# Where a two-layer trunk reduces its modulation weights, and when it draws its gate matmuls

## The chip, the cores and the metric

The program runs on one core of one Trainium2 chip. The metric is the device time of one execution in microseconds (us). The engines of the core are TensorE (PE in the rows), VectorE (DVE), ScalarE (ACT), GpSimd (POOL) and SyncE (SP), which issues the DMA transfers. Each engine runs its own instructions in a fixed order and waits at an instruction until what it needs is there.

## The reference

A trunk of two layers runs over 256 context tokens and 256 latent tokens of width 1024. In each layer the tokens are normalized and modulated, projected by `w_in`, and go through four mixers: grouped attention, a Hyena mixer (two gated long convolutions with filters from a small network), a pooling mixer and a gMLP mixer. Each mixer's result is projected back to the model's width, multiplied by a sigmoid gate that is itself a projection of the tokens, and added up; `w_out` and a SwiGLU feed-forward follow. Shifts, scales and gates of the modulation are a product of a vector with `w_mod`.

```python
mod = (act_lat @ w_mod[l] + b_mod[l])[:, None, :]
sh1, s1, g1, sh2, s2, g2 = jnp.split(mod, 6, axis=-1)
...
p = modulate(x, norm1_w[l], sh1, s1) @ w_in[l]
q = apply_rope(attn_q(p[..., Q_OFF:K_OFF], q_norm_w[l]), cos, sin)
...
# long_conv, twice in the Hyena mixer
uf = jnp.fft.rfft(u.astype(jnp.float32), n=2 * n, axis=1)
y = jnp.fft.irfft(uf * kf[None], n=2 * n, axis=1)[:, :n]
...
merged = (g[..., 0, :] * (attn_out @ lp['w_br_attn'])
          + g[..., 1, :] * (hy @ lp['w_br_hyena'])
          + g[..., 2, :] * (pl @ lp['w_br_pool'])
          + g[..., 3, :] * (gm @ lp['w_br_gmlp']))
x = x + g1 * (merged @ lp['w_out'])
x = x + g2 * swiglu(modulate(x, norm2_w[l], sh2, s2), ffn_w_gate[l], ffn_w_up[l], ffn_w_down[l])
```

The last layer uses its context tokens only for keys and values, so its other work runs over 256 tokens.

## The kernel before

All tokens stay on the chip, with the features on the partitions. The weights are streamed once, in units of 128 x 1024 numbers (512 KB). A product in fp32 is made of three matmuls: each operand is split into a high part and a low part, and `mm3` (L209 to L211) adds high x high, high x low and low x high in one accumulator, over 512 columns in layer 0 and mostly 256 in layer 1. For a weight unit, `load_next` issues a DMA of `raw` on SP's queue, ScalarE casts the high part `whi` (L171) and VectorE subtracts the low part `wlo` (L174). There are five raw buffers and four each of `whi` and `wlo`; a raw buffer is free for the next load when its unit has been split.

`unit_order` lists every unit in the order in which it is streamed, and with it the order of the work. In each layer come the wide units of keys, values and gMLP, ten narrow units (Hyena and pooling), then the gates. `gates(b, js)` gives for the mixer b and each of eight row blocks the gate unit `w_nar` and the projection `w_br`. The wide units of the queries stand between the gates of the gMLP mixer (3) and the others (2, 1, 0). Then come `w_out` (8 units) and the feed-forward in two halves: 22 units of `w_ff` (gate and up), 11 of `w_dn` (down).

The modulation is not computed on TensorE, but for a few chunks. Most of it is made of tiles `w_t`, units of 128 x 1024 too, which `mod_tile` multiplies with a broadcast vector and reduces on VectorE (L259), twice per tile, once for the context and once for the latent tokens. The function `mix(units, tiles)` spreads the tiles evenly between other units. `TILES0` (28 tiles of layer 0: the factor of the first residual, 16 to 23, and most of the feed-forward's modulation) lies in the gate stretch of layer 0, 68 units; `TILES1` (44 tiles of layer 1) lies in layer 0's feed-forward, between its sixth unit and the last four. A tile takes one of the five raw buffers until its reduces are done. The reduces keep the program's order among themselves.

Beside the main line of matmuls run generators. The gates are such a generator (`fill`), and `pump(n)` draws n halves of them (12 matmuls for a half of a gate unit in layer 0) at every `yield` of another generator, so that TensorE has work while the others wait for VectorE and ScalarE. `hyena_gen` draws `HRATE` at each `yield`: it makes the forward transforms (`psU`), the products with the filters' spectra (`ya`, `yb`, L1074 to L1076, split to `yh`, `yl` by L142 and L143), and the inverse transforms (`psiv`), for each of two orders. The query phase draws `QRATE[l]` in each of its steps: `q_gen` normalizes and turns the queries (`qr`, L782) and transposes them on TensorE (`psqT`, L827). `spectra_gen(1)` makes the spectra of layer 1's filters beside the last eight row blocks of layer 0's `w_dn`: exponentials, windows (`fo`, `fs`, `fd`, `fa`), their sum (`pstot`), a reciprocal (L508), products with it (L519), and transforms (`pssp`) of the split results (`fh`, `fl`).

`residual` (L1242) multiplies a finished row block (`pmk`, `pmd`) by its modulation and adds it to `x`, in two halves; `acc` (L322) gathers squares for the next norm.

Each engine's order is written by a scheduler that takes the program, the buffers and its own estimates of durations; the kernel itself fixes the order in which units are loaded and tiles are reduced.

Of the kernel before, what the change touches and what calls it, by code (L numbers as in the profile page):

```python
# [20 lines left out]
KT = D // P  # L21
# [21 lines left out]
BUB = (4, 1)  # L43
REST = 1

HRATE = (1.0, 1.0)
QRATE = (1.4, 1.3)
ARATE = (0.7, 1.4)
QN = (3, 4)
LAG = (1, 2)  # L50
# [2 lines left out]

TILES0 = [(0, i) for i in (*range(16, 24), *range(24, 40), *range(44, 48))]
TILES1 = [(1, i) for i in (*range(40), *range(44, 48))]
MODT = TILES0 + TILES1
CHUNKS = [(0, (8 + i, 9 + i, i, i + 1)) for i in range(0, 8, 2)]
CHUNKS += [(l, tuple(range(4 * c, 4 * c + 4))) for l, c in ((0, 10), (1, 10))]  # L60
# [6 lines left out]
def unit_order():  # L67


    def mix(units, tiles):  # L70
        r, n = [], 0
        for i, u in enumerate(units):
            r.append(u)
            while n * len(units) < (i + 1) * len(tiles):
                r.append(("w_t", MODT.index(tiles[n])))
                n += 1
        return r

    o = []
    for l in range(DEPTH):  # L80
        def gates(b, js):
            return [(n, l, j + (10 + b * KT if n == "w_nar" else 0)) for j in js for n in ("w_nar", f"w_br{b}")]

        o += [("w_wide", l, 0, u) for u in range(4)]
        o += [("w_nar", l, i) for i in range(10)]
        mid = gates(3, range(KT)) + [("w_wide", l, 1, u) for u in range(4)]
        mid += gates(2, range(KT)) + gates(1, range(KT)) + gates(0, range(KT))
        if l == 0:
            mid = mix(mid, TILES0)
        o += mid  # L90
        o += [("w_out", l, j) for j in range(KT)]
        ff = []
        for half in range(2):
            ff += [("w_ff", l, i, half * NFH + f) for f in range(NFH) for i in range(2)]
            ff += [("w_dn", l, half, u) for u in range(NFH)]
        if l == 0:
            ff = ff[:6] + mix(ff[6:-4], TILES1) + ff[-4:]
        o += ff
    return o
# [3 lines left out]
def trunk_kernel(ctx: ExitStack, tc: tile.TileContext, I, out: bass.AP):  # L103
# [543 lines left out]
    o = bank("ss")  # L647
# [7 lines left out]
    for l in range(DEPTH):  # L655
# [364 lines left out]
        def hyena_gen():  # L1020
# [32 lines left out]
            for od in range(2):  # L1053
# [5 lines left out]
                for f in range(2):  # L1059
                    us = []  # L1060
                    for im in range(2):
                        o = side("U")
                        col = im * 256 + f * P
                        for k in range(2):
                            h, lo = fwd[k]
                            mm3(
                                o[:, CS], h[:, col : col + P], lo[:, col : col + P],
                                ut[k][0][:, CS], ut[k][1][:, CS], k == 0, k == 1,
                            )
                        us.append(o)  # L1070
                    kc = "C0" if f == 0 else "A1"
                    for im, (ka, kb_, op) in enumerate(((f"A{f}", f"B{f}", ALU.subtract), (f"B{f}", kc, ALU.add))):
                        a, b = t2(s="ya"), t2(s="yb")
                        V.tensor_mul(seqs(a), seqs(us[0]), kb(ka))  # L1074
                        V.tensor_mul(seqs(b), seqs(us[1]), kb(kb_))
                        V.tensor_tensor(a[:, CS], a[:, CS], b[:, CS], op=op)  # L1076
                        hi, lo = t2(F32R, "yh"), t2(F32R, "yl")
                        split(hi[:, CS], lo[:, CS], a[:, CS])
                        ysp[2 * im + f] = (hi, lo)
                    yield  # L1080
                    yield
                order = (0, 2, 1, 3)
                if od == 0:
                    nut = []
# [46 lines left out]
            qs[t] = t2(s="qs")  # L1131
            S.copy(qs[t], os_[t])
        qg = q_gen()
        for _ in range(len(tts) + QN[l]):
            next(qg, None)
            pump(QRATE[l])

        att = {}

# [387 lines left out]
```

## Time and profile before

| | us |
|---|---|
| median of 3 runs | 1329.41 |
| lowest, highest | 1328.41, 1329.69 |
| profiled execution | 1328.54 |
| its span in the profile | 1326.0 |
| TensorE busy | 1292.9 |
| VectorE busy | 935.6 |
| ScalarE busy | 608.6 |

The rows further down are read so. A busy row gives for each engine the busy time, its share of the span and the number of instructions. A row of the waits names the engine and the operation that waited, the line, the engine and line that released it, the time in all, the times and the longest. A row of the windows gives a stretch, its length, then the busy time (and the count) of PE, PEld, DVE, ACT and POOL, the granted TensorE clock as a share of full speed, the busy share of the DMA engines, and GB/s. A row of a timeline gives start and duration, engine, line, operation, result and operands, shape and count, and in brackets the idle time before it and who ended it. Matmuls overlap: the time from one start to the next is what one costs.

### The profile page before, as it was taken

Reading aid. Unit: us, or ns where it says so; the run is one execution under the profiler, and the core shown is the slowest. Engines: PE = TensorE matmul, PEld = TensorE weight load, DVE = VectorE, ACT = ScalarE, POOL = GpSimd, SP = SyncE. Lnnn points to the kernel's source line nnn. Section 1 sums busy time; section 2 is a strip of 40 time slices with the busy share of each in tenths; the row PEclk is TensorE's granted clock in tenths of the full one; section 3 lists DMA queues with packets and bytes.
Section 4 is the critical chain, followed back from the end, with each engine's and each line's share of the span. In section 5 each row is a group of like instructions: output and inputs, shape, how many; then the busy total and the mean of one; then the engine's idle time right before and its main releaser. Section 6 shows DMA issues by size and latency. Waiting matters only on the chain.

```text
span 1326.0 us, 19996 instructions
## 1 busy us (share of the span) xinstructions
PE 1292.9 (98%) x7714; PEld 1128.2 (85%) x7714; DVE 935.6 (71%) x1599; ACT 608.6 (46%) x1060; POOL 61.9 (5%) x69
## 2 busy tenths in 40 slices
PE   4999999999999999999999999999999999999997
PEld 3778788888888887888888888889989999999997
DVE  3687788798987356666667767966889876655554
ACT  3564333367753246222222224365468854543443
POOL 0000500300000000000000000001210000000000
PEclk7999999999999999999999999999999999999999
DMA  9532334343245552554555554424434457455551
GB/s 343 210 127 77 104 104 143 126 143 112 93 157 160 174 209 73 173 164 159 174 174 175 182 168 143 159 80 128 134 110 139 151 192 247 159 179 188 179 187 49
DMA packets 68063, 203.85 MB, mean 154 GB/s; under 512 B 7552, under 2 KB 13824, under 8 KB 67968
## 3 DMA queue, kind: packets, MB, share of 16 engines
q1 hardware_dynamic: 67968, 202.58, 46.1%
q8 instruction: 60, 0.98, 0.3%
q14 instruction: 35, 0.29, 0.1%
HBM read 201.50 MB, written 1.05 MB: 153 GB/s over the span
## 4 chain that ended last, share of the span: by engine, by line
PE 75%; issue 16%; DVE 5%; ACT 2%; POOL 1%; DMA 0%; DVEq 0%; POOLq 0%; ACTq 0%
PE pmn L209 14%; PE pmn L211 14%; PE pmn L210 14%; PE pmd L209 3%; PE pmd L210 3%; PE pmd L211 3%; PE pmb L209 2%; PE pmb L210 2%; PE pmb L211 2%; PE pmw L676 2%; PE pmw L678 2%; PE pmw L677 2%; PE psav L1188 1%; PE pspt L1166 1%; DVE wlo L174 1%
## 5 line engine op out<-in xcount | busy, mean ns | idle before, releaser
L171 ACT CAST whi<-raw 128x1024 fp32r<-128x1024 f32 (+2 forms) x312 | 288.1, 929 | 470.8 <-PE pmn L210 214.4
L209 PE MATMUL pmn<-hh,whi 128*128 128x512 f32 (+1 forms) x1328 | 449.9, 339 | 0.3 <-DVE vst L721 0.3
L210 PE MATMUL pmn<-hl,whi 128*128 128x512 f32 (+1 forms) x1328 | 448.1, 337 | 0.0
L211 PE MATMUL pmn<-hh,wlo 128*128 128x512 f32 (+1 forms) x1328 | 447.7, 337 | 0.3 <-DVE wlo L174 0.3
L174 DVE TENSOR_TENSOR wlo<-raw,whi 128x1024 fp32r<-128x1024 f32 (+2 forms) x312 | 335.7, 1078 | 143.3 <-ACT whi L171 141.0
L211 PEld LDWEIGHTS pmn<-hh,wlo 128*128 128x128 f32 x1328 | 252.0, 190 | 27.7 <-issue 1.1
L209 PEld LDWEIGHTS pmn<-hh,whi 128*128 128x128 f32 x1328 | 252.1, 190 | 27.6 <-issue 0.9
L210 PEld LDWEIGHTS pmn<-hl,whi 128*128 128x128 f32 x1328 | 252.1, 190 | 26.0 <-issue 0.7
L259 DVE CUSTOM_DVE_ANT_0 junk<-raw,cb,pack_a 128x1024 bf16<-128x1024 f32 x144 | 187.0, 1299 | 1.4
L209 PE MATMUL pmd<-hh,whi 128*128 128x512 f32 (+1 forms) x352 | 119.2, 339 | 0.0
L210 PE MATMUL pmd<-hl,whi 128*128 128x512 f32 (+1 forms) x352 | 118.7, 337 | 0.0
L211 PE MATMUL pmd<-hh,wlo 128*128 128x512 f32 (+1 forms) x352 | 118.0, 336 | 0.0
L210 PEld LDWEIGHTS pmd<-hl,whi 128*128 128x128 f32 x352 | 66.8, 190 | 7.2 <-issue 0.5
L211 PEld LDWEIGHTS pmd<-hh,wlo 128*128 128x128 f32 x352 | 66.8, 190 | 7.1 <-issue 0.2
L209 PEld LDWEIGHTS pmd<-hh,whi 128*128 128x128 f32 x352 | 66.8, 190 | 7.1 <-issue 0.2
L1314 DVE TENSOR_TENSOR sg<-sg,pmn 128x512 f32<-128x512 f32 (+1 forms) x42 | 23.3, 554 | 65.0 <-PE pmn L211 65.0
L345 POOL TENSOR_TENSOR rs<-rs,halfexp 128x4 f32<-128x4 f32 (+1 forms) x5 | 4.4, 884 | 956.9 <-DVE rs L343 956.9
L676 PE MATMUL pmw<-whi,hh 128*128 128x512 f32 (+1 forms) x112 | 43.8, 392 | 3.8 <-ACT hh L389 3.8
L677 PE MATMUL pmw<-wlo,hh 128*128 128x512 f32 (+1 forms) x112 | 42.5, 380 | 0.0
L678 PE MATMUL pmw<-whi,hl 128*128 128x512 f32 (+1 forms) x112 | 42.4, 382 | 0.0
L387 ACT ACTIVATE nh<-nt,mod,amod 128x256 f32<-128x256 f32 x51 | 28.0, 594 | 24.4 <-DVE nt L377 19.2
L1242 DVE SCALAR_TENSOR_TENSOR x<-pmd,mod,x 128x256 f32<-128x256 f32 x48 | 21.8, 476 | 24.5 <-PE pmd L211 24.5
(275 smaller groups left out, 1872.7 us busy)
## 6 DMA issues: line engine op xcount, KB each, us to landing
raw<-in_w_ff SPq DMA_DIRECT2D x88, 512.0 KB, 4.3
raw<-in_w_nar SPq DMA_DIRECT2D x84, 512.0 KB, 3.5
raw<-in_w_t SPq DMA_DIRECT2D x72, 512.0 KB, 3.6
raw<-in_w_dn SPq DMA_DIRECT2D x44, 512.0 KB, 4.2
raw<-in_w_mod SPq DMA_DIRECT2D x48, 256.0 KB, 6.0
raw<-in_w_wide SPq DMA_DIRECT2D x16, 512.0 KB, 3.6
raw<-in_w_out SPq DMA_DIRECT2D x16, 512.0 KB, 3.9
raw<-in_w_br SPq DMA_DIRECT2D x48, 128.0 KB, 2.2
```

The lines of the kernel that those rows point to most:

```text
L171: S.copy(hi[:, :n], raw[:, :n])
L174: V.tensor_sub(lo[:, :n], raw[:, :n], f32(hi[:, :n]))
L209: T.matmul(o, lhsT=wh, rhs=xh, start=first, stop=False)
L210: T.matmul(o, lhsT=wh, rhs=xl, start=False, stop=False)
L211: T.matmul(o, lhsT=wl, rhs=xh, start=False, stop=last)
L259: r = V.tensor_tensor_reduce(out=junk, in0=raw, in1=cb[:, s, :], scale=1.0, scalar=bmod[:, l, i : i + 1], op0=ALU.mult, op1=ALU.add, accum ...
L387: S.activation(h[:, a0:a1], t[:, a0:a1], AF.Identity, bias=sh, scale=a[:, j, k : k + 1])
L676: T.matmul(os_[t][:, :n], lhsT=hh[:, sl], rhs=wh, start=(kt == 0), stop=False)
L677: T.matmul(os_[t][:, :n], lhsT=hh[:, sl], rhs=wl, start=False, stop=False)
L678: T.matmul(os_[t][:, :n], lhsT=hl[:, sl], rhs=wh, start=False, stop=(kt == 7))
L1242: V.scalar_tensor_tensor(x[j][:, sl], o[:, sl], mod[l][:, gi * 8 + j, k : k + 1], x[j][:, sl], op0=ALU.mult, op1=ALU.add)
L1314: V.tensor_mul(sg[:, CS], sg[:, CS], o[:, CS])
```

## The change

Four places are edited. `TILES0` keeps 24 tiles of layer 0 (16 to 39); the tiles 44 to 47 move to the head of `TILES1`, which now has 48, in the same stretch of the feed-forward. Of the 24, 18 are mixed into the gate stretch of layer 0, which now begins behind the gates of the gMLP mixer (52 units: the queries' wide units and the gates 2, 1 and 0), and six (34 to 39) go into `w_out`, two behind each of its third, fourth and fifth units. `hyena_gen` yields once more behind the second product of the first order, in both layers. `QRATE` has one value for the first steps of the query phase and one for the rest; it is 1.4 and 1.4 in layer 0 as before, and 2.0 and then 0.6 in layer 1 instead of 1.3.

```diff
--- before.py
+++ after.py
@@ -43,8 +43,9 @@
 BUB = (4, 1)
 REST = 1
 
+
 HRATE = (1.0, 1.0)
-QRATE = (1.4, 1.3)
+QRATE = ((1.4, 1.4), (2.0, 0.6))
 ARATE = (0.7, 1.4)
 QN = (3, 4)
 LAG = (1, 2)
@@ -53,8 +54,8 @@
 
 
 
-TILES0 = [(0, i) for i in (*range(16, 24), *range(24, 40), *range(44, 48))]
-TILES1 = [(1, i) for i in (*range(40), *range(44, 48))]
+TILES0 = [(0, i) for i in range(16, 40)]
+TILES1 = [(0, i) for i in range(44, 48)] + [(1, i) for i in (*range(40), *range(44, 48))]
 MODT = TILES0 + TILES1
 CHUNKS = [(0, (8 + i, 9 + i, i, i + 1)) for i in range(0, 8, 2)]
 CHUNKS += [(l, tuple(range(4 * c, 4 * c + 4))) for l, c in ((0, 10), (1, 10))]
@@ -83,12 +84,14 @@
 
         o += [("w_wide", l, 0, u) for u in range(4)]
         o += [("w_nar", l, i) for i in range(10)]
-        mid = gates(3, range(KT)) + [("w_wide", l, 1, u) for u in range(4)]
+        o += gates(3, range(KT))
+        mid = [("w_wide", l, 1, u) for u in range(4)]
         mid += gates(2, range(KT)) + gates(1, range(KT)) + gates(0, range(KT))
+        outs = [("w_out", l, j) for j in range(KT)]
         if l == 0:
-            mid = mix(mid, TILES0)
-        o += mid
-        o += [("w_out", l, j) for j in range(KT)]
+            mid = mix(mid, TILES0[:18])
+            outs = outs[:2] + mix(outs[2:5], TILES0[18:]) + outs[5:]
+        o += mid + outs
         ff = []
         for half in range(2):
             ff += [("w_ff", l, i, half * NFH + f) for f in range(NFH) for i in range(2)]
@@ -1079,6 +1082,8 @@
                         ysp[2 * im + f] = (hi, lo)
                     yield
                     yield
+                    if f and od == 0:
+                        yield
                 order = (0, 2, 1, 3)
                 if od == 0:
                     nut = []
@@ -1131,9 +1136,9 @@
             qs[t] = t2(s="qs")
             S.copy(qs[t], os_[t])
         qg = q_gen()
-        for _ in range(len(tts) + QN[l]):
+        for i in range(len(tts) + QN[l]):
             next(qg, None)
-            pump(QRATE[l])
+            pump(QRATE[l][i >= len(tts) + 1])
 
         att = {}
```

The lines behind the edits shift by three to five: L174 becomes L177, L259 becomes L262, L1242 becomes L1247. How the orders move is seen at three places. The first is VectorE in layer 0, between the forward transforms (`psU`) and the inverse ones, whose input is `yh` and `yl`. An ISA row is a modulation tile's reduce, and the 128x1 row behind it reads its accumulator. The kernel before:

```order
L174 TENSOR_TENSOR wlo_307_1429<-raw_285_1345,whi_306_1428 128x1024
L259 ISA junk_87,mod0_88<-raw_303_1416,cb_86,pack_a_76 128x1024
L259 ISA mod0_88 128x1
L1074 TENSOR_TENSOR ya_289_1362<-psU_287_1348,spec_199_922 128x512
L259 ISA junk_87,mod0_88<-raw_303_1416,cb_86,pack_a_76 128x1024
L259 ISA mod0_88 128x1
L1075 TENSOR_TENSOR yb_290_1363<-psU_288_1355,spec_207_950 128x512
L174 TENSOR_TENSOR wlo_323_1497<-raw_308_1432,whi_322_1496 128x256
L1076 TENSOR_TENSOR ya_289_1362<-ya_289_1362,yb_290_1363 128x512
L143 TENSOR_TENSOR yl_292_1368<-ya_289_1362,yh_291_1367 128x512
```

The changed kernel:

```order
L177 TENSOR_TENSOR wlo_303_1411<-raw_281_1328,whi_302_1410 128x1024
L177 TENSOR_TENSOR wlo_308_1427<-raw_286_1343,whi_307_1426 128x256
L1077 TENSOR_TENSOR ya_290_1360<-psU_288_1346,spec_199_922 128x512
L1078 TENSOR_TENSOR yb_291_1361<-psU_289_1353,spec_207_950 128x512
L1079 TENSOR_TENSOR ya_290_1360<-ya_290_1360,yb_291_1361 128x512
L146 TENSOR_TENSOR yl_293_1366<-ya_290_1360,yh_292_1365 128x512
L1077 TENSOR_TENSOR ya_294_1369<-psU_288_1346,spec_207_950 128x512
L1078 TENSOR_TENSOR yb_295_1370<-psU_289_1353,spec_211_968 128x512
L1079 TENSOR_TENSOR ya_294_1369<-ya_294_1369,yb_295_1370 128x512
```

The tile `raw_303` is gone from among the products, and so is the one ahead of these rows; the other instructions keep their order.

The second is VectorE at the end of layer 0's feed-forward, where `x_1029` and `x_1021` are residuals, `rec` the reciprocal, and `wlo_1512` the low half of the eighth unit of the second half's `w_dn`. The kernel before:

```order
L1242 SCALAR_TENSOR_TENSOR x_1029_4357<-pmd_1475_6981,mod0_88,x_1029_4357 128x256 x2
L500 TENSOR_TENSOR fa_1474_6978<-fo_1145_4913 128x256
L174 TENSOR_TENSOR wlo_1512_7172<-raw_1501_7123,whi_1511_7171 128x1024
L322 TENSOR_TENSOR acc_1146_4915<-acc_1146_4915,sq_1483_7033 128x512
L508 RECIPROCAL rec_1485_7039<-pstot_1484_7036 128x512
L259 ISA junk_87,mod1_89<-raw_1479_6996,cb_86,pack_a_76 128x1024
L259 ISA mod1_89 128x1
```

The changed kernel:

```order
L146 TENSOR_TENSOR fl_1499_7105<-fs_1469_6960,fh_1498_7104 128x512
L262 ISA junk_87,mod1_89<-raw_1487_7065,cb_86,pack_a_76 128x1024
L262 ISA mod1_89 128x1
L1247 SCALAR_TENSOR_TENSOR x_1021_4320<-pmd_1500_7108,mod0_88,x_1021_4320 128x256
L262 ISA junk_87,mod1_89<-raw_1487_7065,cb_86,pack_a_76 128x1024
L262 ISA mod1_89 128x1
L325 TENSOR_TENSOR acc_1142_4899<-acc_1142_4899,sq_1505_7154 128x512
L522 TENSOR_TENSOR fd_1459_6892<-fd_1459_6892,rec_1485_7039 128x512
L522 TENSOR_TENSOR fd_1470_6961<-fd_1470_6961,rec_1485_7039 128x512
L177 TENSOR_TENSOR wlo_1512_7172<-raw_1501_7123,whi_1511_7171 128x1024
```

The low half `wlo_1512` has moved from ahead of the reciprocal to behind the last tile and the products with `rec`.

The third is TensorE at the same place. `pmd_1510` is the sixth row block of the down projection, `pmd_1521` and `pmd_1526` the next two. The kernel before:

```order
L210 MATMUL pmd_1510_7167<-hl_1441_6769,whi_1514_7177 128x512
L209 MATMUL pmd_1521_7224<-hh_1326_6087,whi_1514_7177 128x512
L210 MATMUL pmd_1521_7224<-hl_1327_6088,whi_1514_7177 128x512
L209 MATMUL pmd_1526_7269<-hh_1326_6087,whi_1517_7207 128x512
L210 MATMUL pmd_1526_7269<-hl_1327_6088,whi_1517_7207 128x512
L209 MATMUL pssp_1534_7320<-fh_1506_7158,dh_1493_7092 128x512
L210 MATMUL pssp_1534_7320<-fl_1507_7159,dh_1493_7092 128x512
L211 MATMUL pssp_1534_7320<-fh_1506_7158,dl_1494_7093 128x512
L209 MATMUL pssp_1534_7320<-fh_1508_7163,dh_1493_7092 128x512
L209 MATMUL pssp_1539_7341<-fh_1506_7158,dft_fh0_863 128x512
L211 MATMUL pmd_1510_7167<-hh_1440_6768,wlo_1515_7178 128x512
```

The changed kernel:

```order
L213 MATMUL pmd_1510_7167<-hl_1338_6157,whi_1511_7171 128x512
L212 MATMUL pmd_1521_7224<-hh_1324_6079,whi_1514_7177 128x512
L213 MATMUL pmd_1521_7224<-hl_1325_6080,whi_1514_7177 128x512
L212 MATMUL pmd_1526_7269<-hh_1324_6079,whi_1517_7207 128x512
L213 MATMUL pmd_1526_7269<-hl_1325_6080,whi_1517_7207 128x512
L212 MATMUL pssp_1534_7320<-fh_1506_7158,dh_1493_7092 128x512
L212 MATMUL pssp_1539_7341<-fh_1506_7158,dft_fh0_863 128x512
L214 MATMUL pmd_1510_7167<-hh_1337_6156,wlo_1512_7172 128x512
L212 MATMUL pmd_1510_7167<-hh_1350_6233,whi_1511_7171 128x512
L213 MATMUL pmd_1510_7167<-hl_1351_6234,whi_1511_7171 128x512
```

Before, 29 of the sixth block's 33 matmuls stand ahead of the first ones of the next blocks; now five stand there, and the sixth of them, the first that takes `wlo_1512`, comes behind two matmuls of each next block and two transforms.

## Rows read from the trace of the kernel before

**Rows 1.** The page's part 1: busy time, share of the span, count.

```profile
PE 1292.9 (98%) x7714; PEld 1128.2 (85%) x7714; DVE 935.6 (71%) x1599; ACT 608.6 (46%) x1060; POOL 61.9 (5%) x69
```

**Rows 2.** Waits of PE, 140 to 216 us: total, times, longest.

```profile
PE psiv L209 <- ACT yh L142: 1.5, 1, 1.5
```

**Rows 3.** Waits of PE, 900 to 1010 us.

```profile
PE psqT L827 <- DVE qr L782: 1.1, 1, 1.1
PE psiv L209 <- ACT yh L142: 0.6, 1, 0.6
PE pmn L211 <- DVE wlo L174: 0.3, 1, 0.3
```

**Rows 4.** Windows: busy us of PE, PEld, DVE, ACT, POOL, PEclk, DMA, GB/s.

```profile
140.00:200.00 60.00, 58.30 (x264) 48.08 (x263) 51.12 (x80) 20.64 (x38) 14.06 (x11) 1.00 0.31 101
464.00:494.00 30.00, 30.00 (x137) 24.90 (x136) 18.02 (x28) 12.61 (x17) 0.00 (x0) 1.00 0.64 228
520.00:820.00 300.00, 300.00 (x1324) 248.10 (x1323) 205.27 (x291) 86.82 (x106) 0.00 (x0) 1.00 0.52 170
830.00:852.00 22.00, 22.00 (x96) 17.67 (x95) 22.00 (x35) 9.28 (x13) 0.00 (x0) 1.00 0.37 123
```

**Rows 5.** Timeline of PE: start, duration, line, operation, idle before.

```profile
163.52 0.39 PE L211 MATMUL psiv<-yh,dft_il 128*128 128x512 f32 x1
165.38 0.49 PE L209 MATMUL psiv<-yh,dft_ih 128*128 128x512 f32 x1 [1.47 <-ACT yh L142]
...
166.44 0.39 PE L211 MATMUL psiv<-yh,dft_il 128*128 128x512 f32 x1
```

**Rows 6.** Timeline of DVE, w_out's first residual.

```profile
463.81 0.88 DVE L1242 SCALAR_TENSOR_TENSOR x<-pmk,mod,x 128x256 f32<-128x256 f32 x2 [10.38 <-PE pmk L211]
```

**Rows 7.** Timeline of DVE, end of layer 0's feed-forward.

```profile
819.59 0.47 DVE L1242 SCALAR_TENSOR_TENSOR x<-pmd,mod,x 128x256 f32<-128x256 f32 x1
821.22 1.23 DVE L174 TENSOR_TENSOR wlo<-raw,whi 128x1024 fp32r<-128x1024 f32 x1 [1.16 <-ACT whi L171]
...
822.70 1.28 DVE L259 CUSTOM_DVE_ANT_0 junk<-raw,cb,pack_a 128x1024 bf16<-128x1024 f32 x1
823.90 0.08 DVE L259 DVE_READ_ACCUMULATOR2_ANT mod<- 128x1 f32 x1
...
832.13 1.22 DVE L174 TENSOR_TENSOR wlo<-raw,whi 128x1024 fp32r<-128x1024 f32 x1
...
848.89 0.69 DVE L143 TENSOR_TENSOR fl<-fd,fh 128x512 fp32r<-128x512 f32 x1
849.49 1.22 DVE L174 TENSOR_TENSOR wlo<-raw,whi 128x1024 fp32r<-128x1024 f32 x1
850.63 0.69 DVE L143 TENSOR_TENSOR fl<-fd,fh 128x512 fp32r<-128x512 f32 x1
```

**Rows 8.** Timeline of PE, end of layer 0's feed-forward.

```profile
825.66 0.59 PE L506 MATMUL pstot<-fa,ones 128*128 128x512 f32 x1
...
850.05 0.39 PE L209 MATMUL pssp<-fh,dh 128*128 128x512 f32 x1
...
851.18 0.39 PE L211 MATMUL pmd<-hh,wlo 128*128 128x512 f32 x1
```

**Rows 9.** The page's part 6: DMA issues, KB, us to landing.

```profile
raw<-in_w_dn SPq DMA_DIRECT2D x44, 512.0 KB, 4.2
```

**Rows 10.** Timeline of PE, start of the program.

```profile
30.09 0.79 PE L676 MATMUL pmw<-whi,hh 128*128 128x512 f32 x1 [3.27 <-ACT hh L389]
...
33.10 0.39 PE L677 MATMUL pmw<-wlo,hh 128*128 128x512 f32 x1
```

**Rows 11.** Windows: the same columns as rows 4.

```profile
30.00:33.00 3.00, 2.91 (x7) 2.29 (x8) 1.38 (x2) 2.60 (x5) 0.00 (x0) 0.51 1.05 388
165.00:167.00 2.00, 1.39 (x5) 0.95 (x6) 1.64 (x3) 2.00 (x5) 0.00 (x0) 1.00 0.00 0
```

**Rows 12.** Waits of PE, 800 to 880 us.

```profile
PE psrb L360 <- DVE dg L353: 0.8, 1, 0.8
```

## The prediction

> **What bounds the kernel now.** I read the page's first part, then the tensor engine's waits, stretch by stretch, then the busy times of stretches, then the timelines of VectorE and of the tensor engine at the places that the change touches. The first part shows TensorE busy for 98% of the span and VectorE for 71% [rows 1]. The number of matmuls is not changed, so the time can move only by what TensorE stands still for, or by its clock: a stop of TensorE that goes is won in full, one that comes is lost in full.
>
> The list of waits shows few stops that the edits aim at. In layer 0's first inverse transforms TensorE waits 1.5 us for `yh` [rows 2]; in layer 1 it waits 1.1 us for a turned query `qr`, 0.6 us for `yh` and 0.3 us for a low half `wlo` [rows 3]. Against them stand the stretches [rows 4]. VectorE is busy 51.12 of 60 us around the first inverse transforms, 205.27 of 300 us in the body of layer 0's feed-forward, then 22.00 of 22 us where that feed-forward ends and layer 1's filter spectra are made beside it. TensorE is full in the last two. That last stretch has no room on VectorE at all, and the change puts more into it.
>
> **The gain in layer 0's inverse transforms.** Before, one modulation tile (two reduces) stands between the forward transforms and the products `ya`, `yb` from which `yh` is cut; after, there is none, and the extra `yield` draws a gate half of 12 matmuls ahead of the inverse. From the matmul at 163.52 to the one at 166.44 pass 2.92 us for three matmuls [rows 5]; at 0.227 us each (850.05 to 851.18, five matmuls [rows 8]) they would need 0.68. So 2.24 us are lost now. One tile less is 2.4 us less on VectorE, 12 more matmuls are 2.7 us more of cover: 5.1 us against 2.24, so the wait goes whole, with 2.9 us to spare. Next in line there would be the last low part `yl`, which comes just behind `yh` and has the same cover. I take 2.24; ends 1.5 (the named wait alone) and 2.24.
>
> **The gain in layer 1.** The first three of six query steps draw 2.0 instead of 1.3, the rest 0.6. The first transpose of a query stands 42 rows later in TensorE's order than before, and two stand together where one stood alone. I take the 1.1 us for `qr` and the 0.3 us for the `wlo` near it, 1.4 us [rows 3]. The ends: 1.7, with a residue of `qr`'s wait on the matmul's own row, and -0.6, if the thinned second half leaves a later step without cover, by the nearest row, the 0.6 us for `yh`. That wait itself I leave: up to this point the same work stands in front of it on both engines, so the extra `yield` buys nothing in layer 1.
>
> **Tiles in w_out.** Six tiles go there. One reduce goes from start to start in 1.20 us (822.70 to 823.90 [rows 7]), so a tile is 2.4 and six are 14.4 us of VectorE, with six loads of 512 KB on SP's queue. Before the first residual VectorE idles 10.38 us [rows 6]; four tiles, 9.6 us, fit, and the residual starts on time with 0.8 us left. Two follow among the residuals, where VectorE is busy 18.02 of 30 us [rows 4], so 12 us are free for their 4.8. Queued behind them are the low halves of w_out's last units and the loads of the feed-forward's first, which come later by as much. If nothing covers the two, they cost 4.8 - 0.8 = 4.0 us; by the free time I take 0. A gain is excluded there, since TensorE is full in that stretch.
>
> **Tiles in the feed-forward.** Four more tiles share 56 units (48 instead of 44). In the body that is 9.6 us more on a VectorE that is idle for 95 of 300 us [rows 4]; I take 0. The end is the term that decides. Between the second and the third residual of the down projection VectorE's order now has five tiles to come where four stood, and the low half of the eighth unit of `w_dn` (`wlo_1512`), made at 832.13 before the reciprocal in the kernel before, stands behind the reciprocal, all the tiles and the products with the reciprocal.
>
> When will it be done? Before, from the second residual's end, about 820.06, to the end of `wlo_1515`, 850.63 [rows 7], VectorE works without a pause but for 1.16 us before 821.22. After, up to the end of `wlo_1512`, it has the same work with one tile more (+2.4) and the small `amod` (+0.1, by the 0.08 us of a tile's accumulator read at 823.90), with `wlo_1515` left behind (-1.14, 849.49 to 850.63) and one `fl` (-0.60, 848.89 to 849.49). The pause stays: without `wlo_1503` in front of the tile VectorE is early and waits for the third residual's matmuls, which end near 825.7 [rows 8]. 850.63 + 2.4 + 0.1 - 1.14 - 0.60 = 851.4. The loads confirm the order of size: the raw slot of tile 1451 is freed at about 823.4 (820.06, the tile's 2.4 and two small instructions of at most 0.6 each) and brings its `w_dn` unit 4.2 us later [rows 9], at 827.6, when VectorE has just done the third residual; so the loads add little.
>
> When does TensorE want it? In the kernel before, 33 matmuls of the sixth row block stand ahead of the `pssp` at 850.05 [rows 8], so the block begins at 850.05 - 33 x 0.227 = 842.56. After, only five of it, four of the next two blocks and two `pssp` stand ahead of the first matmul with `wlo_1512`: 842.56 + 11 x 0.227 = 845.06. Behind that matmul waits all of the engine's queue, since it runs in order. So TensorE stands 851.4 - 845.06 = 6.4 us. In the kernel before it didn't stand there at all. The ends: 5.5, with VectorE quicker by a residual's wait, and 7.9, with the loads late.
>
> After the stop the clock counts. After a stop of 3.27 us the seven matmuls from 30.09 to 33.10 took 3.01 us instead of 1.59, 1.4 us more, at a granted clock of 0.51; after the 1.47 us at 165.38 it stayed 1.00 [rows 5, 10, 11], which are the levels of 1.2 and 2.4 GHz. A stop of over 5 us is nearer to the first: 1.4 us, ends 0 and 1.4.
>
> The Trainium skill (TensorE: Matmul & The Clock Gate, What's actually happening) says that the slow level is the engine's default and that activity releases it, so that a stop is paid twice, once as idle time and once in slow matmuls behind it. The start of this trace agrees with 0.51; by a rule without that second payment the sum would be 1.4 us less.
>
> Given back: after the stop TensorE is late by 6.4 and VectorE by some 2.5 us, so the 0.8 us that `psrb` waits for `dg` a little later [rows 12] go: -0.8, ends 0 and -0.8.
>
> **The sum.** -2.24 - 1.4 + 6.4 + 1.4 - 0.8 = +3.4 us on the profiled execution's 1328.54 (span 1326.0 and 2.5 around it): 1331.9. The median of the runs lies 0.87 above the profiled execution, so 1332.8 on its scale.
>
> **Rivals.**
> First, VectorE keeps up at the feed-forward's end, and only gains are left: -2.24 - 1.4 = -3.6, 1325.8, with the `yh` wait of layer 1 gone too 1325.2. For it: tiles leave a stretch with 51.12 of 60 busy for one with 205.27 of 300, and no tensor wait stands at the end now. Against it: the 22.00 of 22. It decides the case if `wlo_1512` is done by 845.1, 6.3 us earlier than my tally.
> The Trainium skill (Perfetto Trace Analysis, Optimization Strategy) says that interleaving regimes with different busiest engines may pay; by it alone this rival is what happens. The trace agrees for the whole feed-forward, and not for its end.
> Second, only the work that is really added there is paid, one tile: +2.4 - 3.6 = -1.2, 1328.2. For it: sum of work on VectorE is the same but for that tile. Against it: the place of `wlo_1512` makes TensorE wait for work that it needed later before, not only for the tile.
> Third, w_out: tile loads of 512 KB are late, the tiles hold VectorE past 463.81, the first residual and the low halves behind it come late, and TensorE stands before its next row block. Price 4.0 us, from the point at which the fourth tile ends after 463.81: 1332.8 + 4.0 = 1336.8. For it: the margin is 0.8 us. Against it: there are four accumulator banks, so the residual's is not wanted at once, and the 12 us that are free behind it.
>
> **How the numbers follow.** About 0.2%, 2.7 us, is what a measurement can tell from no change: faster is under 1326.7, slower over 1332.1. The forecast has 0.60; its own range is 1330.2 to 1336.8 (gains 0.9 to 3.9, loss 4.7 to 9.3, so +0.8 to +8.4, of which the last point, all bad ends at once, is cut), of which 0.46 is slower, as the clock and `psrb` terms mostly cancel, and 0.14 no change. The first rival has 0.18 (0.14 faster, 0.04 no change), the second 0.14 (0.13 no change, 0.01 faster), the third 0.08, slower. Together faster 0.15, same 0.31, slower 0.54. The range 1325.5 to 1336.8 takes in the first rival's plain gain and the third's price.
>
> **What would show it.** Right: the 1.5 us of `yh` in layer 0 gone from TensorE's waits; the `qr` wait gone or under 0.5; around 840 to 850 a wait of TensorE for a `wlo` or `fh`, of 5 to 8 us in all, with the granted clock under 1 behind it; VectorE full from 823 to 855; `wlo_1512` after the reciprocal and the tiles. Wrong: TensorE full there, with the low half done ahead of it; or a wait in w_out before 470, where I have none; or the `yh` wait still there with VectorE idle ahead of it, which would mean that something else than the tile held `yh`.

## The result, and the profile after

The changed kernel takes 1335.9 us (median of 5 runs, 1335.54 to 1336.11) against 1329.41 us before (5 runs, 1328.41 to 1330.00). The ratio is 1.0052, with a 95% interval of 1.0038 to 1.0066: slower by 6.5 us, inside the range and on the forecast side, but by nearly twice the predicted 3.4 us. The profiled execution took 1335.9 us with a span of 1334.1, which is 8.1 us more than the span before. The medians differ by less, for two reasons: the median before is 0.9 above its profiled execution, and the time outside the span is 1.8 us now where it was 2.5.

The page's first part, which answers to [rows 1], and the windows that answer to [rows 4] (same columns):

```profile
PE 1295.3 (97%) x7714; PEld 1128.0 (85%) x7714; DVE 936.1 (70%) x1599; ACT 609.8 (46%) x1060; POOL 58.1 (4%) x69
```

```profile
140.00:200.00 60.00, 60.00 (x266) 49.67 (x266) 42.73 (x75) 19.75 (x36) 12.32 (x11) 1.00 0.25 81
464.00:494.00 30.00, 30.00 (x134) 24.86 (x133) 22.69 (x36) 12.53 (x16) 0.00 (x0) 1.00 0.83 279
520.00:820.00 300.00, 300.00 (x1323) 248.06 (x1322) 212.51 (x301) 87.70 (x107) 0.00 (x0) 1.00 0.55 175
830.00:852.00 22.00, 15.63 (x68) 12.03 (x66) 21.53 (x34) 8.07 (x12) 0.00 (x0) 0.97 0.41 131
```

The number of matmuls is the same, and so is VectorE's work. VectorE has more time around the first inverse transforms (42.73 us, 51.12 before) and more to do in the body of the feed-forward (212.51, 205.27 before), where TensorE stays full. In the last stretch TensorE has lost 6.4 of 22 us. The waits of TensorE say on whom, in layer 0's query phase, at the feed-forward's end and in layer 1 (these answer to [rows 3] and [rows 12]; the wait of [rows 2] is gone):

```profile
PE psqT L830 <- DVE qr L785: 1.2, 1, 1.2
PE pmn L214 <- DVE wlo L177: 0.4, 2, 0.2
```

```profile
PE pssp L212 <- ACT fh L145: 6.4, 1, 6.4
```

```profile
PE pmb L212 <- ACT th L966: 1.3, 1, 1.3
PE psiv L212 <- ACT yh L145: 0.9, 1, 0.9
```

The start of the n-th matmul in one trace less the start of the n-th in the other gives a ledger. At the end of the start-up the changed kernel is 0.3 us late; behind layer 0's inverse transforms 2.0 early; behind its attention 0.8 late; from there to the end of the feed-forward's body it stays 0.8 late; at the start of layer 1 it is 9.4 late, behind its query phase 9.5, and from 1140 us on 8.1. So the inverse transforms won 2.3; the stretch from there to the end of the attention, most of it the query phase, gave all of it back and half a microsecond more; the end of the feed-forward lost 8.6; and 1.4 came back late in layer 1, as told at the end.

The feed-forward's end in TensorE's timeline, and the granted clock behind the stop:

```profile
845.13 0.40 PE L213 MATMUL pmd<-hl,whi 128*128 128x512 f32 x1
851.90 0.79 PE L212 MATMUL pssp<-fh,dh 128*128 128x512 f32 x1 [6.37 <-ACT fh L145]
852.49 0.63 PE L212 MATMUL pssp<-fh,dft_fh 128*128 128x512 f32 x1
852.99 0.79 PE L214 MATMUL pmd<-hh,wlo 128*128 128x512 f32 x1
853.58 0.63 PE L212 MATMUL pmd<-hh,whi 128*128 128x512 f32 x1
...
856.99 0.56 PE L214 MATMUL pmd<-hh,wlo 128*128 128x512 f32 x1
857.38 0.39 PE L212 MATMUL pmd<-hh,whi 128*128 128x512 f32 x1
```

```profile
845.00:852.00 7.00, 0.63 (x3) 0.19 (x2) 6.71 (x12) 3.74 (x7) 0.00 (x0) 0.89 0.37 118
852.00:857.00 5.00, 5.00 (x12) 3.54 (x13) 5.00 (x6) 0.45 (x1) 0.00 (x0) 0.50 0.57 183
857.00:862.00 5.00, 5.00 (x23) 4.11 (x22) 1.33 (x2) 1.05 (x1) 0.00 (x0) 0.97 0.80 290
```

TensorE stops for 6.37 us. The twelve matmuls from 851.90 to 857.38 then take 5.48 us where 2.72 would do, at a granted clock of 0.50. VectorE's timeline at the same place (compare [rows 7]):

```profile
833.75 3.35 DVE L511 RECIPROCAL rec<-pstot 128x512 f32<-128x512 f32 x1
...
848.70 1.27 DVE L262 CUSTOM_DVE_ANT_0 junk<-raw,cb,pack_a 128x1024 bf16<-128x1024 f32 x1
849.90 0.08 DVE L262 DVE_READ_ACCUMULATOR2_ANT mod<- 128x1 f32 x1
849.90 0.69 DVE L325 TENSOR_TENSOR acc<-acc,sq 128x512 f32<-128x512 f32 x1
850.51 1.29 DVE L522 TENSOR_TENSOR fd<-fd,rec 128x512 f32<-128x512 f32 x2
851.71 1.22 DVE L177 TENSOR_TENSOR wlo<-raw,whi 128x1024 fp32r<-128x1024 f32 x1
852.85 1.29 DVE L146 TENSOR_TENSOR fl<-fd,fh 128x512 fp32r<-128x512 f32 x2
```

The reciprocal is at the same time as before, but what had stood ahead of it, the low half at 851.71, now follows everything else. It did not wait for its data: ScalarE began to cast the high half of the same unit 17.7 us earlier, as soon as the unit had landed:

```profile
833.98 1.05 ACT L174 CAST whi<-raw 128x1024 fp32r<-128x1024 f32 x1 [3.70 <-DMA raw<-in_w_dn]
```

The wait itself ends with `fh`; the low half is done one microsecond later, just as the two `pssp` are through, and costs no wait of its own.

### The profile page after: what moved, and what is told of

It is laid out like the page before. It is cut to its first block, busy times and chain, and to the rows that moved or that the text cites. A ratio compares the mean times of both kernels' runs of the same rounds, so it can differ in the third digit from the quotient of the medians.

```text
span 1334.1 us, 19988 instructions
## 1 busy us (share of the span) xinstructions
PE 1295.3 (97%) x7714; PEld 1128.0 (85%) x7714; DVE 936.1 (70%) x1599; ACT 609.8 (46%) x1060; POOL 58.1 (4%) x69
## 4 chain that ended last, share of the span: by engine, by line
PE 73%; issue 16%; DVE 7%; ACT 2%; POOL 1%; DMA 1%; DVEq 0%; POOLq 0%; ACTq 0%
PE pmn L214 15%; PE pmn L212 15%; PE pmn L213 14%; PE pmd L214 2%; PE pmd L213 2%; PE pmd L212 2%; PE pmb L212 2%; PE pmb L214 2%; PE pmb L213 2%; PE psav L1193 1%; PE pmw L679 1%; DVE junk L262 1%; PE pmw L681 1%; PE pmw L680 1%; PE pspt L1171 1%
## 5 line engine op out<-in xcount | busy, mean ns | idle before, releaser
L174 ACT CAST whi<-raw 128x1024 fp32r<-128x1024 f32 (+2 forms) x312 | 288.8, 929 | 461.6 <-PE pmn L213 213.6
L177 DVE TENSOR_TENSOR wlo<-raw,whi 128x1024 fp32r<-128x1024 f32 (+2 forms) x312 | 336.3, 1081 | 163.6 <-ACT whi L174 161.7
L262 DVE CUSTOM_DVE_ANT_0 junk<-raw,cb,pack_a 128x1024 bf16<-128x1024 f32 x144 | 184.2, 1279 | 1.4
L1247 DVE SCALAR_TENSOR_TENSOR x<-pmd,mod,x 128x256 f32<-128x256 f32 x48 | 21.9, 477 | 22.0 <-PE pmd L214 22.0
```

Source lines behind the costliest of these rows:

```text
L174: S.copy(hi[:, :n], raw[:, :n])
L177: V.tensor_sub(lo[:, :n], raw[:, :n], f32(hi[:, :n]))
L262: r = V.tensor_tensor_reduce(out=junk, in0=raw, in1=cb[:, s, :], scale=1.0, scalar=bmod[:, l, i : i + 1], op0=ALU.mult, op1=ALU.add, accum ...
L1247: V.scalar_tensor_tensor(x[j][:, sl], o[:, sl], mod[l][:, gi * 8 + j, k : k + 1], x[j][:, sl], op0=ALU.mult, op1=ALU.add)
```

## The experiments

Every run is beside runs of the kernel before on the same chip; times are medians, and each ratio is to that kernel, with its 95% interval.

**Is it the feed-forward's end, and only that?** In e1 the tiles end earlier:

```diff
-            ff = ff[:6] + mix(ff[6:-4], TILES1) + ff[-4:]
+            ff = ff[:6] + mix(ff[6:-12], TILES1) + ff[-12:]
```

> The changed kernel with one edit: the 48 tiles of the feed-forward are mixed so that none stands among its last 12 units (before: the last 4). Theory: the stop of TensorE at the end of layer 0's feed-forward comes from tiles that stand on VectorE ahead of the low half wlo_1512; without tiles there the stop (6.5 us) and the slow matmuls behind it (about 3 us) go, so 8 to 9.5 us less than the changed kernel: 1326.5 to 1328, no wait of TensorE between 820 and 860. Rival 1, four more tiles in the feed-forward cost wherever they stand (loads and raw buffers): 1334 to 1336. Rival 2, tiles that are packed denser make a new stop in the body: over 1330, with a wait of pmn or pmd for wlo before 820.

Measured: 1329.31 us (before 1328.66), 1.0009 (1.0000 to 1.0018). The stop is gone, and the loss with it but for 0.6 us; the forecast of 1326.5 to 1328 was too low. Two small stops have come in the body, where the tiles are denser, which is the run's second rival in small, though not for a `wlo`. By the ledger they cost 1.8 us. The waits of this kernel, 520 to 800 us:

```profile
PE pmd L213 <- DVE hl L1321: 0.8, 1, 0.8
PE pmd L212 <- ACT hh L1320: 0.4, 1, 0.4
```

In e2 the change's edit of the feed-forward's tiles stands alone, on the kernel before:

```diff
-TILES0 = [(0, i) for i in (*range(16, 24), *range(24, 40), *range(44, 48))]
-TILES1 = [(1, i) for i in (*range(40), *range(44, 48))]
+TILES0 = [(0, i) for i in range(16, 40)]
+TILES1 = [(0, i) for i in range(44, 48)] + [(1, i) for i in (*range(40), *range(44, 48))]
```

> The kernel before with one edit: the tiles 44 to 47 of layer 0 go from the gate stretch to the head of the feed-forward's tiles (48 there, 24 in the gate stretch, none in w_out, no extra yield, the old query rate). Theory: the whole loss is in this edit, 8 to 9.5 us more than the kernel before, less what a thinner gate stretch wins (0 to 2.2): 1335.5 to 1339, with a stop of about 6.4 us of pssp for fh. Rival 1, only the added tile's work is paid: 1330 to 1332. Rival 2, the stop needs the tiles in w_out as well (loads late by some us): no stop here, 1327 to 1330.

Measured: 1333.76 us (before 1328.66), 1.0038 (1.0025 to 1.0051). The stop is there without the tiles in w_out, so it does not need them, and it costs far more than a tile. In time the loss is under the forecast: 1.5 us of it are hidden by the ledger, since the thinner gate stretch has lost the `yh` wait, and the runs that were not profiled (1333.28 and up) are faster than the profiled one (1335.85). The wait, 800 to 890 us:

```profile
PE pssp L209 <- ACT fh L142: 6.2, 1, 6.2
```

In e3 the change has the four tiles back in the gate stretch:

```diff
-TILES0 = [(0, i) for i in range(16, 40)]
-TILES1 = [(0, i) for i in range(44, 48)] + [(1, i) for i in (*range(40), *range(44, 48))]
+TILES0 = [(0, i) for i in (*range(16, 34), *range(44, 48), *range(34, 40))]
+TILES1 = [(1, i) for i in (*range(40), *range(44, 48))]
...
-            mid = mix(mid, TILES0[:18])
-            outs = outs[:2] + mix(outs[2:5], TILES0[18:]) + outs[5:]
+            mid = mix(mid, TILES0[:22])
+            outs = outs[:2] + mix(outs[2:5], TILES0[22:]) + outs[5:]
```

> The changed kernel with the tiles 44 to 47 back in the gate stretch of layer 0 (22 of them there, 6 in w_out, 44 in the feed-forward). Theory: VectorE's order at the end of the feed-forward is that of the kernel before, so the stop goes; what is left are the gains in layer 0's inverse transforms (2.2) against what the query phase of layer 0 gave back (2.1) and the small changes in layer 1: 1326 to 1329.5. Rival, the tiles in w_out are part of the loss: 1331 or more.

Measured: 1328.47 us (before 1328.66), 0.9997 (0.9988 to 1.0006). No stop at the feed-forward's end, and no gain either: the six tiles in w_out are free, and layer 0's query phase, with a wait of 1.3 us for a `wlo`, eats what the inverse transforms won.

**Is it the place of one low half, or the load?** In e6 one unit more than in the change is without tiles:

```diff
-            ff = ff[:6] + mix(ff[6:-4], TILES1) + ff[-4:]
+            ff = ff[:6] + mix(ff[6:-5], TILES1) + ff[-5:]
```

> The changed kernel with the 48 tiles of the feed-forward mixed up to the last 5 units instead of the last 4. Behind the second residual VectorE now has four tiles instead of five, and the low halves of the seventh and eighth w_dn unit stand ahead of the reciprocal. Theory, the place of the eighth low half makes the stop: it goes with the slow matmuls behind it, 6 to 9 us less than the changed kernel, 1327 to 1330 where that has 1335.9. Rival, VectorE's load makes it (one tile of 2.4 us less): 1333 to 1334, with a stop of some 4 us left.

Measured: 1327.73 us (before 1328.97), 0.9993 (0.9984 to 1.0002). VectorE has one tile less there, 2.4 us, and the time goes from 6.5 us over the kernel before to no difference that can be told from it, which one tile's load can't explain. Its timeline before the reciprocal, and the one wait that TensorE has left between 800 and 900 us:

```profile
832.12 1.23 DVE L177 TENSOR_TENSOR wlo<-raw,whi 128x1024 fp32r<-128x1024 f32 x1
...
834.80 1.23 DVE L177 TENSOR_TENSOR wlo<-raw,whi 128x1024 fp32r<-128x1024 f32 x1
...
837.14 3.36 DVE L511 RECIPROCAL rec<-pstot 128x512 f32<-128x512 f32 x1
```

```profile
PE pstot L509 <- DVE fa L503: 0.5, 1, 0.5
```

Two low halves now stand ahead of the reciprocal. The reciprocal is 3.3 us later than in the kernel before, four tiles still follow the second residual, and no stop comes of it. So the place decides, and the prediction's second rival, that only the added tile is paid, is wrong. (The scheduler's order on TensorE moves with it: all `pssp` stand behind the sixth row block again.)

**Where did the gain of layer 0 go?** In e4 the extra `yield` stands alone, on the kernel before:

```diff
                     yield
                     yield
+                    if f and od == 0:
+                        yield
```

> The kernel before with the extra yield alone. Theory: 12 matmuls more, 2.7 us of cover against 2.24 us of excess, so the wait for yh in layer 0 goes although the tile still stands between; the query phase then meets VectorE earlier and gives some of it back: 1327 to 1329. Rival, it is the tile's absence that removes the wait: the wait stays at 1 us or more and the time at 1329 to 1330.

Measured: 1326.05 us (before 1328.66), 0.9980 (0.9970 to 0.9989). The wait for `yh` is gone with the tile still in its place, and nothing is given back, so the time is below the range that was expected. In e7 the new query rate is added, and no tile is moved:

```diff
-QRATE = (1.4, 1.3)
+QRATE = ((1.4, 1.4), (2.0, 0.6))
...
-            pump(QRATE[l])
+            pump(QRATE[l][i >= len(tts) + 1])
```

> The kernel before with the extra yield and the new query rate, and no tile moved. Theory: the yield's gain of 2 to 3 us stays whole and the rate does nothing, 1326 to 1327.5 where the kernel before has 1329.4; no wait for qr of over 0.5 us in layer 0's query phase. Rival, the gain in the inverse transforms is given back in layer 0's query phase whatever the tiles do: 1328.5 to 1329.5, with a wait for qr in layer 0.

Measured: 1326.02 us (before 1328.97), 0.9978 (0.9969 to 0.9987): the same. So it is the tiles' moves that make layer 0's query phase wait. Which of them? In e8, beside the yield, six tiles go into w_out, and the rest stay mixed from the gMLP gates on:

```diff
-TILES0 = [(0, i) for i in (*range(16, 24), *range(24, 40), *range(44, 48))]
+TILES0 = [(0, i) for i in (*range(16, 34), *range(44, 48), *range(34, 40))]
...
-            mid = mix(mid, TILES0)
-        o += mid
-        o += [("w_out", l, j) for j in range(KT)]
+            mid = mix(mid, TILES0[:22])
+        outs = [("w_out", l, j) for j in range(KT)]
+        if l == 0:
+            outs = outs[:2] + mix(outs[2:5], TILES0[22:]) + outs[5:]
+        o += mid + outs
...
```

> The kernel before with the extra yield and with the tiles 34 to 39 moved from the gate stretch into w_out (22 tiles are left in the gate stretch, still mixed from the gMLP gates on; the feed-forward as before). Theory: tiles in w_out are free, and with tiles still taken beside the long convolutions the query phase has no more of them than before: 1325.5 to 1327.5 where the kernel before has 1329.4. Rival 1, w_out's tiles cost up to 4 us: over 1329 with a wait between 455 and 495. Rival 2, any yield with a thinner gate stretch is given back in the query phase: a wait for qr or wlo of over 1 us between 255 and 270.

Measured: 1328.18 us (before 1328.97), 0.9997 (0.9988 to 1.0006). My theory fell here, the second rival held: w_out is free, but `qr` is waited for again (1.2 us), though the stretch has fewer tiles and they begin where they did. In the changed kernel two tiles lie on VectorE among the query steps:

```profile
241.45 0.69 DVE L765 TENSOR_TENSOR qn<-qs,ss 128x512 f32<-128x512 f32 x1 [0.93 <-POOL ss L757]
...
242.78 1.28 DVE L262 CUSTOM_DVE_ANT_0 junk<-raw,cb,pack_a 128x1024 bf16<-128x1024 f32 x1
...
244.11 1.28 DVE L262 CUSTOM_DVE_ANT_0 junk<-raw,cb,pack_a 128x1024 bf16<-128x1024 f32 x1
...
249.86 1.28 DVE L262 CUSTOM_DVE_ANT_0 junk<-raw,cb,pack_a 128x1024 bf16<-128x1024 f32 x1
...
251.18 1.28 DVE L262 CUSTOM_DVE_ANT_0 junk<-raw,cb,pack_a 128x1024 bf16<-128x1024 f32 x1
...
252.39 0.69 DVE L765 TENSOR_TENSOR qn<-qs,ss 128x512 f32<-128x512 f32 x1
...
258.83 0.52 DVE L785 TENSOR_TENSOR qr<-qr,qt 128x256 f32<-128x256 f32 x1
```

```profile
257.94 0.27 PE L830 MATMUL psqT<-pack_a,qr 128*128 128x128 f32 x1
259.41 0.33 PE L830 MATMUL psqT<-pack_a,qr 128*128 128x128 f32 x1 [1.20 <-DVE qr L785]
```

Here and in e8 four reduces, 4.8 us, run between the first query's `qn` and the third's; in e7 it is one tile, two reduces from 248.83. It looks as if the two tiles hold up the fourth `qr`, but e7 says otherwise:

```profile
242.25 0.69 DVE L762 TENSOR_TENSOR qn<-qs,ss 128x512 f32<-128x512 f32 x1 [0.93 <-POOL ss L754]
...
259.47 0.42 DVE L782 TENSOR_TENSOR qr<-qr,qt 128x256 f32<-128x256 f32 x1
```

```profile
258.73 0.27 PE L827 MATMUL psqT<-pack_a,qr 128*128 128x128 f32 x1
258.76 0.48 PE L209 MATMUL pmn<-hh,whi 128*128 128x512 f32 x1
...
259.94 0.33 PE L827 MATMUL psqT<-pack_a,qr 128*128 128x128 f32 x1
```

From the start of the first `qn` to the end of the fourth `qr` VectorE takes 17.9 us in the changed kernel and in e8, and 17.6 in e7 and in the kernel before: it pauses more in those, and most of the second tile fits into the pauses. TensorE reaches the third transpose 16.5 us behind that `qn` in all four, so it doesn't come early for it either. What differs is TensorE's order. In e7 four matmuls, 0.9 us, stand between the third transpose and the fourth; in the changed kernel and in e8 the fourth stands right behind the third. So some 0.3 of the 1.2 us is the tiles' load, and 0.9 is the order that the scheduler wrote around them. Spreading fewer tiles evenly had moved two of them into that gap, and TensorE's order changed with them. If so, keeping them out should bring the old order back, as in e9:

```diff
-            mid = mix(mid, TILES0[:18])
+            mid = mid[:10] + mix(mid[10:], TILES0[:18])
...
-            ff = ff[:6] + mix(ff[6:-4], TILES1) + ff[-4:]
+            ff = ff[:6] + mix(ff[6:-5], TILES1) + ff[-5:]
```

> The changed kernel with the feed-forward's tiles mixed up to the last 5 units, and with the 18 tiles of the gate stretch beginning ten units later, so that none stands among the query steps of layer 0. Theory: the wait for qr in layer 0 (1.2 us, 1.9 with what follows it) comes from two tiles that stand on VectorE among the query steps, not from how many tiles the stretch has; it goes, and the time is 1.5 to 2.2 us under the same kernel without the shift: 1325.5 to 1327 where the kernel before has 1329. Rival, TensorE simply arrives earlier than VectorE can deliver: a wait for qr of over 0.8 us is left and the time is 1327.5 to 1329.

Measured: 1326.53 us (before 1328.76), 0.9981 (0.9972 to 0.9989). The wait for `qr` is gone, and the four matmuls stand between the transposes again. Against e6, the same kernel without the shift (0.9993 to the kernel before), that is some 1.6 us, though the two intervals just overlap. Not all of the gain stays: by the ledger 0.9 of the 2.3 us that the inverse transforms won are lost by the end of the attention, which e4, e7 and e11 don't lose. Between 216 and 450 us TensorE has one wait, there:

```profile
PE pspt L1171 <- ACT pe L1162: 0.5, 1, 0.5
```

**The query rate of layer 1.** In e5 the rate stands alone, on the kernel before:

```diff
-QRATE = (1.4, 1.3)
+QRATE = ((1.4, 1.4), (2.0, 0.6))
...
```

> The kernel before with the new query rate alone (2.0 then 0.6 in layer 1). Theory from the changed kernel's trace: the wait for qr (1.1 us) goes, but a wait of a gate matmul for th (1.3 us) comes in its place when the rate drops, so no change: 1328.5 to 1330 where the kernel before has 1329.4. Rival, my prediction's term: 1.4 us are won, 1327.5 to 1328.3.

Measured: 1328.12 us (before 1328.97), 0.9994 (0.9985 to 1.0003): no change that can be told. The interval goes from 2.0 us faster to 0.4 slower, so the time alone doesn't exclude the 1.4 us; the trace does. By the ledger 1.3 us are won where `qr` was waited for and 1.3 lost where the rate drops:

```profile
PE pmb L209 <- ACT th L963: 1.3, 1, 1.3
```

In e10 two edits in layer 1 come on top of e9:

```diff
-QRATE = ((1.4, 1.4), (2.0, 0.6))
+QRATE = ((1.4, 1.4), (2.0, 1.0))
...
-                    if f and od == 0:
+                    if f and od == 0 and l == 0:
```

> The kernel of the run beside it with two more edits in layer 1: no extra yield there, and the second query rate 1.0 instead of 0.6. Theory: the yield does nothing in layer 1 (its yh wait stays at 0.6 to 0.9 us) and the gate matmul waits for th when the rate drops; a rate of 1.0 makes that wait 0 to 1 us, so 0 to 1.5 us less than beside it: 1324.5 to 1327. Rival, the wait only moves to qr or wlo: the same time within 0.5 us.

Measured: 1324.29 us (before 1328.76), 0.9965 (0.9952 to 0.9978), the lowest median of all. Waits of TensorE from 890 to 1010 us:

```profile
PE psiv L212 <- ACT yh L145: 0.6, 1, 0.6
PE pmn L214 <- DVE wlo L177: 0.3, 1, 0.3
PE psU L212 <- DVE ul L146: 0.3, 1, 0.3
```

Neither `qr` nor `th` is waited for any more; `yh` is back at 0.6 us, where it was before the extra yield. By the ledger layer 1's part up to its second norm is 0.8 us shorter than in the kernel before, where e9 is 0.1 longer. The two edits can be told apart by other runs: e4, with the yield and the old rate, waits 0.9 us for `th` and loses 0.3 us there by the ledger, so in layer 1 the yield does some harm; e11 below differs from e5 in layer 1 by the rate alone, and has no wait for `th`.

**Are the tiles' moves worth anything?** e11 is e10 without a moved tile:

```diff
 # the kernel before, with
+QRATE = ((1.4, 1.4), (2.0, 1.0))
...
+                    if f and od == 0 and l == 0:
+                        yield
...
```

> The kernel before with the extra yield in layer 0 alone and with layer 1's query rate 2.0 then 1.0, and no tile moved. Theory: TensorE has no wait left that the tiles' places could remove, so the tiles' moves are worth nothing and this is as fast as the same kernel with the tiles moved: 1324 to 1325.2 where the kernel before has 1329. Rival, thinner tiles beside the long convolutions, and the end of the feed-forward without psrb's wait, are worth some 0.5 to 1.5 us: 1325 to 1326.

Measured: 1324.98 us (before 1328.72), 0.9975 (0.9965 to 0.9985). And e12 is e10, tiles and all, without the yield:

```diff
-                    if f and od == 0 and l == 0:
-                        yield
```

> The version with all tiles moved and shifted (feed-forward up to the last 5 units, gate stretch ten units later, layer 1's rate 2.0 then 1.0) without the extra yield. Theory: with no tile beside the products VectorE delivers yh early enough by itself, so the wait for yh in layer 0 stays away without the yield: under 0.5 us there, 1324 to 1325.5. Rival, the yield's 12 matmuls are what covers it, whatever the tiles do: a wait of 1 us or more, and 1326 to 1327.

Measured: 1325.49 us (before 1328.72), 0.9976 (0.9967 to 0.9986); no wait at layer 0's inverse transforms. The intervals of e10, e11 and e12 overlap: the yield alone or the tiles' absence alone removes the `yh` wait, and the moved tiles bring nothing that these runs can tell. The ledger has them losing 0.8 us in layer 0's attention (e10 against e11) and winning 0.7 at the feed-forward's end. What the three differ by, about a microsecond, stays open.

## Why the prediction was right, and where it was not

*The end of the feed-forward* was right in mechanism and in size. The forecast had TensorE stop for 6.4 us at the first matmul with `wlo_1512`. The stop is 6.37 us; from the last start before it to the first behind it are 6.54 us more than the 0.227 that a matmul takes. `wlo_1512` starts at 851.71 and is done by 852.9; TensorE was 0.8 us late by then, so that is 852.1 in the time of before, for 851.4 forecast. In one detail the forecast missed: it let the two `pssp` run ahead of the stop, but `fh` was late too, by the same queue on VectorE, and the stop ends when `fh` is there. (Its 33 matmuls ahead of `pssp` in the kernel before are 29 of the sixth block and four of the next two, not 33 of the sixth; the sum is the same.) Ending the tiles earlier (e1, e6) takes the stop away, adding them alone (e2) makes it.

*The clock behind the stop* was mis-sized. The forecast took 1.4 us from the seven matmuls at the program's start; here twelve matmuls ran at 0.50 and cost 2.76 us more. The term's upper end was 1.4 as well; that the loss of 8.6 lies within the forecast 4.7 to 9.3 is owed to the width of the stop's term. The Trainium skill (TensorE: Matmul & The Clock Gate, What's actually happening) has the slow level as the default that activity releases; the 0.50 behind this stop agrees, and this stop was paid twice, as idle time and as slow matmuls.

*`psrb`* was right in size: its wait went, 0.7 us by the ledger. The reason that the forecast gave, TensorE's lateness after the stop, isn't shown. The wait is gone in e1, e6, e9, e10 and e12 too, which have no stop; it is there in every trace with 44 tiles in the feed-forward and in none with 48.

*Layer 0's inverse transforms* were right: 2.3 us won for 2.24, no wait left. The forecast counted the tile and the yield together; each alone is enough (e4, e12).

*"A stop of TensorE that goes is won in full"* failed. The forecast looked for the next wait at the same place and not one phase later. In the changed kernel 2.8 us are lost between the inverse transforms and the end of the attention, 1.8 of them in waits that the trace names: 1.2 for `qr`, 0.4 for `wlo`, 0.2 for `mg`. That TensorE arrives 2 us earlier is not the reason, since in e4 and e7 it does so too and loses nothing. The tiles' new spacing put two of them among the query steps, and the scheduler's order for TensorE changed with it. All of the gain went there in the changed kernel, in e3 and most of it in e8; it stays whole in e4 and e7, which move no tile, and 1.4 of it in e9.

*Layer 1's query* failed in its sum: 1.4 us were won where they were forecast, by the changed kernel's ledger, and 1.3 were lost again for `th` where the rate falls to 0.6, so that nothing is left. The forecast had named this, a later step without cover, as the lower end of the term, and taken none of it. With a rate of 1.0 both waits are gone (e10, e11). That the extra `yield` does nothing in layer 1 was wrong as well: `yh` is waited for 0.9 us instead of 0.6 in every trace that has it there.

*w_out* and *the body of the feed-forward* cost nothing, as forecast: the ledger stays at 0.8 from 360 to 820 us. VectorE still comes 1.24 us early to the first residual, where it had 10.38 before [rows 6]:

```profile
464.61 0.88 DVE L1247 SCALAR_TENSOR_TENSOR x<-pmk,mod,x 128x256 f32<-128x256 f32 x2 [1.24 <-PE pmk L214]
```

The third rival, late tiles in w_out, did not come about. Nor did the first, a VectorE that keeps up: over the body it does (212.51 of 300), and the loss is at the end, where a share over the whole stretch says nothing.

So the sum of the forecast, -2.24 - 1.4 + 6.4 + 1.4 - 0.8, reads in the profile 0.3 at the start, -2.3, +2.8, +8.6 and +0.1, and then -1.4 from the clock late in layer 1: 8.1. The gains, forecast at 0.9 to 3.9, came to a loss of 0.6. So the side was right because the largest term was; that the time still lies in the range is in part luck, since the gains were outside theirs and the 1.4 us that came back were in no term.

## What to carry to other kernels

Work moved off a full engine helps only where someone waited for it, and it does harm where it lands ahead of something small that is due: look at the order on the receiving engine at the landing place, not at its busy share over the stretch, and at the order of the engine that waits, which a scheduler rewrites when filler moves. An even spread of filler moves every piece when one number changes, so after each change look at the places with little slack, here the queries and the last row blocks, and keep filler out of them by name. A gain at one wait must be followed to the next meeting of the same two engines before it is booked.

## What the runs showed of the hardware

The same stop does not always cost the same clock. At the second norm of layer 1 TensorE waits 1.1 us for `hh` in every kernel. The two microseconds behind it in the kernel before, then in the changed one (columns as in rows 4):

```profile
1124.55:1126.55 2.00, 2.00 (x11) 2.00 (x12) 1.82 (x6) 1.76 (x4) 0.00 (x0) 0.66 0.40 160
```

```profile
1134.05:1136.05 2.00, 2.00 (x15) 1.98 (x16) 1.83 (x6) 1.75 (x4) 0.00 (x0) 1.00 0.34 137
```

Of the fourteen traces of this study ten kept 1.00 there and four fell to 0.53 to 0.72. In before against after this is the 1.4 us that the ledger gives back, with no instruction changed there. What decides it was not tried. The start-up, which no edit aims at, varies too: it ends 0.1 to 1.5 us later in the other thirteen traces than in that of the kernel before. So one profile's span against another's says little below 2 us, and the ledger, stretch by stretch, says more.
